# Sums of squares from rows of tokens on ScalarE, and their reciprocal roots spread by products with a diagonal

## The chip, the core and the metric

The kernel runs on one core of one Trainium2 chip. A core has TensorE (PE, with its weight loads PEld), VectorE (DVE), ScalarE (ACT), GpSimd (POOL) and SyncE (SP), which work side by side and wait for each other by semaphores. SP issues nearly all transfers between the memory of the chip (HBM) and the core's own memory. The metric is the device time of one execution in microseconds (us); a kernel's time is the median of its runs.

## The reference

One decoder layer on 512 tokens with 16 learned meta tokens ahead of them, 528 rows of 2048 numbers in float32. What matters here is its first step and what uses it:

```python
def rmsnorm(x, gain):
    xf = x.astype(jnp.float32)
    y = xf * lax.rsqrt(jnp.mean(xf * xf, axis=-1, keepdims=True) + EPS)
    return (y * gain.astype(jnp.float32)).astype(x.dtype)

def hybrid_layer(h, g_pre, w_in, w_gate_up, b_gate, g_gla_out, w_conv, w_out, g_post):
    xn = rmsnorm(h, g_pre)
    p = xn @ w_in
    q, k, v, z_gla, r, hc, gate_b, gate_c, z_conv = jnp.split(p, SPLIT_POINTS, axis=-1)
    ...                      # gated linear attention on q, k, v, r; convolution on the rest
    y = jnp.concatenate([y_gla, y_conv], axis=-1) @ w_out
    return h + rmsnorm(y, g_post)
```

So every token needs one number, the reciprocal root of the mean square of its row of 2048.

## The kernel before

**Layout.** Activations stand transposed: the 2048 features lie on 128 partitions in 16 tiles (k-tiles), the 528 tokens along the free dimension. The input xT comes in that form, and x comes a second time by rows for the residual at the end. Each operand of a product is split into an upper and a lower half, hi and lo, and three products (hi hi, hi lo, lo hi) make one of float32 accuracy. A weight block of 8 k-tiles is a granule: it is loaded into one of five raw buffers, ACT casts the upper half (L145, later L124) and DVE makes the lower (L146, later L125). There are three buffers each for the halves.

**The opening stage.** The loop at L664 loads xT in pieces (`XCUT`: two single k-tiles, then pairs), and the weights of k0 and q0 in between (`WCUT`). For each k-tile ACT writes the upper half of x times the gain (L670, into xa for k-tiles 0 to 7 and xb for 8 to 15) and DVE the lower (L671). For each piece ACT squares the raw tile (L692, L695) and DVE adds it to an accumulator of two tiles (L696). The loop at L697 multiplies k0, q0 and the 16 columns of r for each k-tile. Behind k-tile 10 in the code stands the sum over the partitions: four products of the accumulator with a matrix of ones (L710), which leave the sum of each token's squares on every partition. ACT takes the root of the mean (L711), DVE the reciprocal (L712), and `rstd`, 128 x 528, is the factor of each token on all partitions.

**What needs rstd.** The columns of k, q and r are multiplied by it as DVE takes them out of PSUM (`normal`, L723); r goes through three more steps (L763 to L765). Then DVE normalises the sixteen tiles of xT themselves (L776) while PE does v0, v1, z0 and z1 on the plain halves. From the normalised tiles DVE and ACT make sums and differences of blocks (L783, L788, L789), the operands of the block products (seven instead of eight for a pair of columns) that fill the rest of the kernel. The first pair is z2z3. Its weight blocks are added by DVE (L200, L230) and split (L124, L125).

**What sets the order.** The program is written as one stream, and a scheduling layer orders the instructions of each engine when it is built; the engine then runs its list in that order. Transfers on SP and ACT share eight semaphores in turn: each transfer waits until the one eight before it has landed. SP works in order, so a load that waits holds up those behind it.

**Names.** `scr` is the scratch area that holds the accumulator and the squares, the raw columns of r and the raw gate weights; `ini` is the pool of the opening stage; `st` are the two PSUM banks of the sums; `ident` is the identity matrix, made at the start for transposes.

Of the kernel before, what the change touches and what calls it, by code (L numbers as in the profile page):

```python
# [27 lines left out]
NP = S // P  # L28
# [3 lines left out]
XHALF = L // 2  # L32
# [10 lines left out]


@with_exitstack
def hymba_kernel(ctx, tc, xT, x, g_pre, w_r, w_t, w_up, b_gate, g_gla, w_conv, w_o, g_post, out):
    nc = tc.nc
    PSUM = bass.MemoryType.PSUM

# [12 lines left out]
    def mm(out_, lhsT, rhs, start, stop, **kw):  # L62
        nc.tensor.matmul(out_, lhsT, rhs, start=start, stop=stop, **kw)  # L63

    V, A, G = nc.vector, nc.scalar, nc.gpsimd


    epst = const.tile([P, 1], F32, name="epst")
# [38 lines left out]
    xa = [xap.tile([P, 2, NB, XHALF], F32R, tag=f"xa{i}", name=f"xa{i}") for i in range(2)]  # L107
    WQ = 4 * NB * P
    wr2 = q0w[:, WQ:WQ + KT * 2 * RANK].rearrange("p (k r) -> p k r", r=2 * RANK)
    acc = scr[:, 0:2 * L].rearrange("p (k t) -> p k t", t=L)  # L110
    sqs = [scr[:, L * (2 + 2 * i):L * (4 + 2 * i)].rearrange("p (k t) -> p k t", t=L)
           for i in range(2)]
# [537 lines left out]
    with tc.tile_pool(name="ini", bufs=1, reuse_waits="tile") as ini:  # L650
# [10 lines left out]
        q0v = q0w[:, 0:WQ].rearrange("p (g s k c) -> p g s k c", g=2, s=2, k=NB)  # L661
        wk = [new_gran(), None]
        wq_ = [(q0v[:, g, 0], q0v[:, g, 1], new_raw()) for g in range(2)]
        for n_, (k0, k1) in enumerate(XCUT):  # L664
            ks = slice(k0, k1)
            nc.sync.dma_start(xr[:, ks, :], xT[:, ks, :])
            for kt in range(k0, k1):
                xt, xk = raw_x(kt)
                src = xr[:, kt, :].rearrange("p (s t) -> p s t", t=XHALF)
                A.activation(xt[0][:, :, xk, :], src, AF.Copy, scale=gp[:, kt:kt + 1])  # L670
                V.scalar_tensor_tensor(out=xt[1][:, :, xk, :], in0=src, scalar=gp[:, kt:kt + 1],  # L671
                                       in1=xt[0][:, :, xk, :].bitcast(F32),
                                       op0=ALU.mult, op1=ALU.subtract)
            for a, b in WCUT.get(k0, ()):
                if a == NB:
                    free(wk[0][2])
                    wk[1] = new_gran()
                fill_gran(wk[a // NB], w_t[TILE["k0"]], a, b)
                fill_gran(wq_[a // NB], w_t[TILE["q0"]], a, b)
            if k0 == 0:  # L680
                A.dma_start(wr_raw, w_r)
                V.tensor_copy(wr2[:, :, 0:RANK], wr_raw)
                V.tensor_tensor(out=wr2[:, :, RANK:], in0=wr_raw,
                                in1=wr2[:, :, 0:RANK].bitcast(F32), op=ALU.subtract)
            if k0 == 8:
                nc.sync.dma_start(wup_raw, w_up)
                nc.sync.dma_start(bg, b_gate)
                G.tensor_scalar(out=nbg, in0=bg, scalar1=-1.0, scalar2=None, op0=ALU.mult)
                nc.sync.dma_start(gg, g_gla)
                nc.sync.dma_start(wc, w_conv)  # L690
            if k0 < 2:
                A.activation(acc[:, k0:k1, :], xr[:, ks, :], AF.Square)  # L692
            else:
                sq = sqs[n_ % 2]
                A.activation(sq, xr[:, ks, :], AF.Square)  # L695
                V.tensor_tensor(out=acc, in0=acc, in1=sq, op=ALU.add)  # L696
        for kt in range(KT):  # L697
            xt, xk = raw_x(kt)
            plain_k(k_ps, wk, kt, 0)
            plain_k(q_ps, wq_, kt, NM // 2)  # L700
            for i in range(2):
                for n in range(2):
                    mm(r_ps[n][0:2 * RANK, 0:XHALF], wr2[:, kt, :], xt[i][:, n, xk, :],
                       kt == 0 and i == 0, kt == KT - 1 and i == 1)
            if kt == 10:
                for n in range(2):
                    t = slice(n * XHALF, (n + 1) * XHALF)
                    st_ = bank(f"st{n}")
                    for i in range(2):
                        mm(st_[:, 0:XHALF], ones, acc[:, i, t], i == 0, i == 1)  # L710
                    A.activation(rstd[:, t], st_[:, 0:XHALF], AF.Sqrt, bias=epst, scale=1.0 / D)  # L711
                V.reciprocal(rstd, rstd)  # L712
        for raw in (wk[1][2], wq_[0][2], wq_[1][2]):
            free(raw)

# [313 lines left out]
def _layout(inp):  # L1029
# [9 lines left out]
    return {  # L1039
        "xT": c(h.T[:, COLS].reshape(KT, P, L).transpose(1, 0, 2)),  # L1040
        "x": c(x),
        "g_pre": c(np.asarray(inp["norm_pre"])[0].reshape(KT, P).T),
        "w_r": c(wk[:, :, 3072:3088].transpose(1, 0, 2)),
        "w_t": c(tiles),
# [24 lines left out]
```

## Time and profile before

| | |
|---|---|
| Median of three runs | 821.43 us (820.8 to 821.86) |
| Profiled execution | 823.31 us, its span 820.8 us |
| PE busy | 794.0 us, 97% |
| DVE busy | 688.4 us, 84% |
| ACT busy | 437.6 us, 53% |
| Chain that ended last | PE 77%, DVE 12%, DMA 4%, ACT 4%, issue 2% |
| DMA queue of SP | 94.73 MB, 35.7% of the span |
| Mean granted clock of TensorE | 0.99 |

The span runs from the first to the last instruction of the core; the profiled execution's own time has a few microseconds around it. The change lies in the first 45 us. In the row of 40 slices of 20.5 us each, the DMA digits of the first two slices are 9 and 5 and then mostly 1 to 3: the opening stage is the part in which the transfers are busy. The chain of work that ended last is followed back from the end; its shares say on which engine the end hung, over the whole program.

### The profile page before, as it was taken

How to read it: one execution, taken by the hardware profiler on the slowest of the kernel's cores; microseconds unless marked ns; L12 is line 12 of the kernel's file. 1: busy time of each engine (PE TensorE's matmuls, PEld its weight loads, DVE VectorE, ACT ScalarE, POOL GpSimd, SP SyncE). 2: the span in 40 equal slices, each digit the busy share in tenths (PEclk: the TensorE clock that was granted, in tenths of full speed). 3: DMA queues.
4: the chain of work that ended last, by engine and by line, in shares of the span. 5: the costliest groups of instructions: out<-in, count | busy, mean ns of one | idle time of the engine just before them, and what ended most of it. 6: DMA issues, size and time to landing. Idle time of an engine off the chain costs nothing.

```text
span 820.8 us, 15178 instructions
## 1 busy us (share of the span) xinstructions
PE 794.0 (97%) x6364; PEld 776.2 (95%) x6364; DVE 688.4 (84%) x820; ACT 437.6 (53%) x638; POOL 3.8 (0%) x15
## 2 busy tenths in 40 slices
PE   9999989999999999999999999999999999999992
PEld 8999989998999999999999999999999889999992
DVE  6999979789697789878887888787879986787887
ACT  7635675685766484644444444444446534444442
POOL 0000000000000000000000000000000000000000
PEclk9999999999999999999999999999999999999996
DMA  9513243234133532253333333333333622333346
GB/s 288 223 52 91 92 129 102 89 119 154 54 103 114 169 99 88 85 193 103 111 105 119 100 116 106 115 102 110 105 115 116 178 77 76 104 101 106 103 161 250
DMA packets 34052, 98.97 MB, mean 121 GB/s; under 512 B 4064, under 2 KB 8800, under 8 KB 33344
## 3 DMA queue, kind: packets, MB, share of 16 engines
q1 hardware_dynamic: 31968, 94.73, 35.7%
q10 hardware_dynamic: 2016, 3.29, 1.2%
q8 instruction: 49, 0.80, 0.4%
q14 instruction: 19, 0.16, 0.1%
HBM read 89.61 MB, written 8.39 MB: 119 GB/s over the span
## 4 chain that ended last, share of the span: by engine, by line
PE 77%; DVE 12%; DMA 4%; ACT 4%; issue 2%; SPq 0%; DVEq 0%; ACTq 0%
PE out L63 5%; PE out3P L63 4%; PE out1P L63 4%; PE out2P L63 3%; PE v L63 3%; PE v2v3P L63 3%; PE h0c0P L63 2%; PE h5c5P L63 2%; PE h2c2P L63 2%; PE h7c7P L63 2%; PE h6c6P L63 2%; PE h4c4P L63 2%; PE h3c3P L63 2%; PE h1c1P L63 2%; PE b0s0P L63 2%; PE b6s6P L63 2%
## 5 line engine op out<-in xcount | busy, mean ns | idle before, releaser
L124 ACT CAST whi<-raw 128x1024 fp32r<-128x1024 f32 x225 | 235.2, 1050 | 256.7 <-DVE raw L200 85.4
L125 DVE TENSOR_TENSOR wlo<-raw,whi 128x1024 fp32r<-128x1024 f32 x225 | 273.7, 1220 | 66.7 <-ACT whi L124 61.5
L200 DVE TENSOR_TENSOR raw<-raw 128x1024 f32<-128x1024 f32 x75 | 90.3, 1219 | 6.6 <-DMA raw<-in_w_t_dram 5.6
L230 DVE TENSOR_TENSOR raw<-raw 128x1024 f32<-128x1024 f32 x25 | 30.5, 1220 | 0.6
L145 ACT CAST whi<-raw 128x1024 fp32r<-128x1024 f32 (+2 forms) x13 | 10.9, 845 | 19.5 <-PE v L63 12.8
L63 PE MATMUL out<-whi,xt 128*128 128x512 f32 x64 | 20.0, 394 | 0.0
L63 PE MATMUL out2P<-whi,xt 128*128 128x256 f32 x96 | 17.2, 282 | 0.4 <-ACT whi L124 0.4
L63 PE MATMUL out3P<-whi,xt 128*128 128x256 f32 x96 | 17.2, 282 | 0.4 <-ACT whi L124 0.4
L63 PE MATMUL out1P<-whi,xt 128*128 128x256 f32 x96 | 17.1, 281 | 0.0
L63 PEld LDWEIGHTS out2P<-whi,xt 128*128 128x128 f32 x96 | 14.7, 188 | 0.6 <-ACT whi L124 0.6
L63 PEld LDWEIGHTS out3P<-whi,xt 128*128 128x128 f32 x96 | 14.7, 188 | 0.6 <-ACT whi L124 0.6
L63 PEld LDWEIGHTS out<-whi,xt 128*128 128x128 f32 x64 | 12.0, 188 | 2.8
L63 PEld LDWEIGHTS out1P<-whi,xt 128*128 128x128 f32 x96 | 14.7, 188 | 0.0
L63 PE MATMUL out2P<-wlo,xt 128*128 128x256 f32 x48 | 13.4, 280 | 0.0
L63 PE MATMUL out3P<-wlo,xt 128*128 128x256 f32 x48 | 13.4, 280 | 0.0
L63 PE MATMUL out1P<-wlo,xt 128*128 128x256 f32 x48 | 13.4, 280 | 0.0
L63 PE MATMUL out<-wlo,xt 128*128 128x512 f32 x32 | 12.6, 394 | 0.0
L146 DVE TENSOR_TENSOR wlo<-raw,whi 128x1024 fp32r<-128x1024 f32 (+2 forms) x13 | 12.5, 965 | 0.0
L605 DVE SCALAR_TENSOR_TENSOR y<-hh,wc,y 128x512 f32<-128x512 f32 x16 | 12.0, 748 | 0.2
L363 ACT ACTIVATE junk<-y 128x256 f32<-128x256 f32 x18 | 7.5, 418 | 8.7 <-DVE y L474 8.4
L63 PE MATMUL out3P<-whi,xb 128*128 128x256 f32 x64 | 11.7, 282 | 0.0
L63 PE MATMUL out2P<-whi,xb 128*128 128x256 f32 x64 | 11.6, 282 | 0.0
(749 smaller groups left out, 2701.3 us busy)
## 6 DMA issues: line engine op xcount, KB each, us to landing
raw<-in_w_t_dram SPq DMA_DIRECT2D x108, 512.0 KB, 4.1
raw<-in_w_o_dram SPq DMA_DIRECT2D x24, 512.0 KB, 4.0
raw<-in_w_o_dram SPq DMA_DIRECT2D x16, 256.0 KB, 3.5
xres<-in_x_dram SPq DMA_DIRECT2D x4, 1024.0 KB, 8.0
xr<-in_xT_dram SPq DMA_DIRECT2D x7, 528.0 KB, 6.9
z<-zd SPq DMA_DIRECT2D x8, 256.0 KB, 3.9
yd<-z SPq DMA_DIRECT2D x8, 256.0 KB, 2.0
yg<-yd SPq DMA_DIRECT2D x1, 2048.0 KB, 10.2
```

What stands on the lines that cost most here:

```text
L63: nc.tensor.matmul(out_, lhsT, rhs, start=start, stop=stop, **kw)
L124: A.copy(hi, raw)
L125: V.tensor_tensor(out=lo, in0=raw, in1=hi.bitcast(F32), op=ALU.subtract)
L145: A.copy(hi[:, k, :], raw[:, k, :])
L146: V.tensor_tensor(out=lo[:, k, :], in0=raw[:, k, :], in1=hi[:, k, :].bitcast(F32), op=ALU.subtract)
L200: V.tensor_tensor(out=a, in0=a, in1=b, op=ALU.add)
L230: V.tensor_tensor(out=raw["11"], in0=raw["11"], in1=raw["22"], op=ALU.subtract)
L363: A.activation(junk, oy["src"], AF.Square, accum_out=fin["ssq"][:, t, n:n + 1])
L605: V.scalar_tensor_tensor(out=y, in0=hh[:, i:i + S], scalar=wc[:, j, i:i + 1], in1=y, op0=ALU.mult, op1=ALU.add)
```

## The change

The squares are no longer taken from the transposed tiles. The rows of x, and the meta tokens as a new input `meta`, are loaded a second time during the opening stage: four tiles of 128 tokens and one of 16, each in two halves of 1024 features, into four buffers in the scratch area in turn. ACT squares each half and sums it along the row in the same instruction (`accum_out`), so the sums lie one token a partition in a 128 x 5 x 2 tile. DVE adds the two halves, ACT takes the root, DVE the reciprocal, all on 128 x 5 numbers. ACT then scales the identity by each column, which gives five diagonal matrices, and PE multiplies them by ones: the product has the factor of each token on every partition, in the order of the columns of xT. ACT copies it from PSUM into `rstd`. The seven additions and the reciprocal on 128 x 528 numbers of DVE, and the four products of the squares with ones, are gone.

```diff
-            if k0 < 2:
-                A.activation(acc[:, k0:k1, :], xr[:, ks, :], AF.Square)
-            else:
-                sq = sqs[n_ % 2]
-                A.activation(sq, xr[:, ks, :], AF.Square)
-                V.tensor_tensor(out=acc, in0=acc, in1=sq, op=ALU.add)
+        def square_rows():
+            if not parts:
+                return
+            t, c = parts.pop(0)
+            n = P if t < NP else NM
+            buf = rows[(2 * t + c) % 4][0:n]
+            src = x[t * P:(t + 1) * P] if t < NP else meta
+            nc.sync.dma_start(buf, src[:, c * DH:(c + 1) * DH])
+            A.activation(buf, buf, AF.Square, accum_out=sums[0:n, t, c:c + 1])
...
+            for _ in range(0 if k0 < 2 else 1 if k0 < 8 else 2):
+                square_rows()
...
-            if kt == 10:
+            if kt == 12:
+                V.tensor_tensor(out=rms, in0=sums[:, :, 0], in1=sums[:, :, 1], op=ALU.add)
+                A.activation(rms, rms, AF.Sqrt, bias=epst, scale=1.0 / D)
+                V.reciprocal(rms, rms)
+                for t in range(NP + 1):
+                    A.activation(diag[:, t, :], ident, AF.Copy, scale=rms[:, t:t + 1])
+            if kt == 14:
                 for n in range(2):
-                    t = slice(n * XHALF, (n + 1) * XHALF)
                     st_ = bank(f"st{n}")
-                    for i in range(2):
-                        mm(st_[:, 0:XHALF], ones, acc[:, i, t], i == 0, i == 1)
-                    A.activation(rstd[:, t], st_[:, 0:XHALF], AF.Sqrt, bias=epst, scale=1.0 / D)
-                V.reciprocal(rstd, rstd)
+                    m = slice(NM // 2, NM) if n == 0 else slice(0, NM // 2)
+                    mm(st_[:, 0:NM // 2], ones[0:NM], diag[0:NM, NP, m], True, True)
+                    for t in range(2):
+                        o = NM // 2 + t * P
+                        mm(st_[:, o:o + P], ones, diag[:, 2 * n + t, :], True, True)
+                    A.copy(rstd[:, n * XHALF:(n + 1) * XHALF], st_[:, 0:XHALF])
```

The scheduling layer sets where this stands on each engine. From the second pair of block products on, the lists of all engines are the same as before. Line numbers of the change are higher by 17 to 20 (L670 is L687, L711 and L712 have become L720 to L732, L723 is L743, L776 is L796).

PE at the end of the opening stage; `st0` and `st1` are the banks of the sums, `v00` and `v01` those of v0. Before:

```order
L63 MATMUL k00_129<-xb1_102,whi_179 128x264
L63 MATMUL k01_130<-xb1_102,whi_179 128x264
L63 MATMUL k00_129<-xb0_101,wlo_180 128x264
L63 MATMUL st0_412<-scr_104,ones_88 128x264 x2
L63 MATMUL st1_416<-scr_104,ones_88 128x264 x2
L63 MATMUL k01_130<-xb0_101,wlo_180 128x264
L63 MATMUL q00_131<-xb0_101,q0w_103 128x256
```

In the change:

```order
L63 MATMUL r0_127<-xb1_102,q0w_103 32x264
L63 MATMUL r1_128<-xb1_102,q0w_103 32x264
L63 MATMUL st0_492<-diag_140,ones_88 128x8
L63 MATMUL st0_492<-diag_140,ones_88 128x128 x2
L63 MATMUL st1_497<-diag_140,ones_88 128x8
L63 MATMUL st1_497<-diag_140,ones_88 128x128 x2
L63 MATMUL v00_559<-xa0_108,whi_521 128x264
```

The sums stood in the middle of k-tile 13; the products with the diagonals stand behind the last product of r for k-tile 15, directly ahead of v0.

ACT from the halving of the last pair of k-tiles on. Before:

```order
L695 ACTIVATE scr<-xr 128x1056
L670 ACTIVATE xb_101<-xr,gp 128x2x264 x2
L695 ACTIVATE scr<-xr 128x1056
L145 CAST whi<-raw 128x1024 x2
L711 ACTIVATE rstd<-st_412,epst 128x264
L711 ACTIVATE rstd<-st_416,epst 128x264
L145 CAST whi<-raw 128x1024
L763 CAST rr<-scr 32x528
```

In the change:

```order
L679 ACTIVATE scr,sums<-scr 16x1024
L687 ACTIVATE xb_101<-xr,gp 128x2x264 x2
L679 ACTIVATE scr,sums<-scr 16x1024
L720 ACTIVATE rms<-rms,epst 128x5
L145 CAST whi<-raw 128x1024
L723 ACTIVATE diag<-ident,rms 128x128 x5
L145 CAST whi<-raw 128x1024
L732 COPY rstd<-st_492 128x264
L732 COPY rstd<-st_497 128x264
L145 CAST whi<-raw 128x1024
L783 CAST rr<-scr 32x528
```

The two weight casts of v0 stood behind the last square and ahead of the roots; now one stands between the root and the diagonals and one between the diagonals and the copies.

SP, the loads from k-tiles 8 and 9 on. In the change (before, the three loads of xr behind wc stand together, with nothing in between):

```order
L683 DMA xr_116<-in_xT_dram 128x1056
L703 DMA scr_104<-in_w_up_dram 96x512
L704 DMA bg_84<-in_b_gate_dram 128x4
L706 DMA gg_86<-in_g_gla_dram 128x2
L707 DMA wc_87<-in_w_conv_dram 128x24
L678 DMA scr_104<-in_x_dram 128x1024 x2
L683 DMA xr_116<-in_xT_dram 128x1056
L678 DMA scr_104<-in_x_dram 128x1024 x2
L683 DMA xr_116<-in_xT_dram 128x1056
L678 DMA scr_104<-in_x_dram 128x1024
L678 DMA scr_104<-in_meta_dram 16x1024
L683 DMA xr_116<-in_xT_dram 128x1056
```

Five parts of x and one of meta stand ahead of loads of xr here, three more parts stand ahead of the first row shown, and the second part of meta follows the last. On DVE, the lower halves of v0's two granules (L146) stand ahead of the normalising of r, k and q in both, with the reciprocal of rstd between them before; r is normalised first in the change, where k was first before.

More of the change, by code (lines that the diff above doesn't have):

```diff
@@ L45, in hymba_kernel @@
 @with_exitstack
-def hymba_kernel(ctx, tc, xT, x, g_pre, w_r, w_t, w_up, b_gate, g_gla, w_conv, w_o, g_post, out):
+def hymba_kernel(ctx, tc, xT, x, meta, g_pre, w_r, w_t, w_up, b_gate, g_gla, w_conv, w_o, g_post, out):
     nc = tc.nc
@@ L109, in hymba_kernel @@
     wr2 = q0w[:, WQ:WQ + KT * 2 * RANK].rearrange("p (k r) -> p k r", r=2 * RANK)
-    acc = scr[:, 0:2 * L].rearrange("p (k t) -> p k t", t=L)
-    sqs = [scr[:, L * (2 + 2 * i):L * (4 + 2 * i)].rearrange("p (k t) -> p k t", t=L)
-           for i in range(2)]
+    DH = D // 2
+    rows = [scr[:, o:o + DH] for o in (0, DH, 2 * DH, 9 * L)]
     wr_raw = scr[:, 6 * L:6 * L + KT * RANK].rearrange("p (k r) -> p k r", r=RANK)
@@ L663, in hymba_kernel @@
         wq_ = [(q0v[:, g, 0], q0v[:, g, 1], new_raw()) for g in range(2)]
+        sums = ini.tile([P, NP + 1, 2], F32, name="sums")
+        rms = ini.tile([P, NP + 1], F32, name="rms")
+        diag = ini.tile([P, NP + 1, P], F32, name="diag")
+        G.memset(sums, 0.0)
+        parts = [(t, c) for t in range(NP + 1) for c in range(2)]
+        def square_rows():
[7 more added lines that the diff above has]
+            A.activation(buf, buf, AF.Square, accum_out=sums[0:n, t, c:c + 1])
         for n_, (k0, k1) in enumerate(XCUT):
@@ L1041, in _layout @@
         "x": c(x),
+        "meta": c(np.asarray(inp["meta_tokens"])),
         "g_pre": c(np.asarray(inp["norm_pre"])[0].reshape(KT, P).T),
```

## The prediction

> **What bounds the kernel now.** I read the page first (PE busy for 97% of the span, so a change in the opening stage counts by what it does to the start of the later ones), then the chain of waits from 36 to 100 us, then the stage's timelines engine by engine.
>
> ```profile
> 40.49 23.49 PE v L63 x192
> ...
> 67.54 2.34 DVE tt L783 x2
> ...
> 98.23 1.05 ACT whi L124
> ...
> 99.33 0.74 PE z2z3P L63 x4
> ```
>
> The chain (start, duration, what) runs on PE while it multiplies v, goes over to DVE at 67.5, and comes back to PE at 99.33 through a weight cast of ACT, which had waited for DVE's block sum (L230). PE waits there, and DVE has had no idle time for 55 us before it:
>
> ```profile
> PE z2z3P L63 <- ACT whi L124: 1.0, 1, 1.0
> 43.50:98.10 54.60, 54.60 (x458) 54.57 (x456) 54.59 (x64) 27.20 (x29) 0.53 (x1) 1.00 0.25 78
> ```
>
> The first row is from the waits between 40 and 100 us (total, times, longest), the second from the table of stretches (PE, PEld, DVE, ACT and POOL busy, clock, DMA share, GB/s). DVE is busy for 54.59 of 54.60 us and PE for all of them. So whatever delays DVE's start on this block arrives undiminished at 99 us, on top of the 1.0 us that PE waits already; a delay of PE alone could be at most as large as that of DVE to stay hidden. Behind 99 us both engines follow the same list as before, so a shift there lasts to the end.
>
> The question is thus when the opening stage hands over: when PE starts v, and when DVE starts the normalising at L723 and L776. Its supply is the queue of transfers on SP:
>
> ```profile
> 10.73 0.51 SPq L666 DMA_DIRECT2D xr<-in_xT_dram  x1
> xr<-in_xT_dram SPq DMA_DIRECT2D x1, 528.0 KB, 9.1
> 15.88 0.33 SPq L666 DMA_DIRECT2D xr<-in_xT_dram  x1
> xr<-in_xT_dram SPq DMA_DIRECT2D x1, 528.0 KB, 6.6
> 18.12 0.33 SPq L666 DMA_DIRECT2D xr<-in_xT_dram  x1
> xr<-in_xT_dram SPq DMA_DIRECT2D x1, 528.0 KB, 7.0
> ```
>
> Each pair of rows is one load of two k-tiles of xT: issue time, and us from issue to landing. Pair 8/9 lands at 19.8, pair 10/11 at 22.5, pair 14/15 at 25.1 us. PE takes them up later:
>
> ```profile
> 22.74 0.40 PE L63 MATMUL k<-xb,whi 128*128 128x264 f32 x2
> 26.59 0.29 PE L63 MATMUL k<-xb,whi 128*128 128x264 f32 x1
> 33.28 2.05 PE L63 MATMUL st<-scr,ones 128*128 128x264 f32 x8
> 34.97 0.48 PE L63 MATMUL k<-xb,wlo 128*128 128x264 f32 x1
> 36.47 0.40 PE L63 MATMUL k<-xb,whi 128*128 128x264 f32 x2
> 40.32 0.41 PE L63 MATMUL v<-xa,whi 128*128 128x264 f32 x2
> ```
>
> Pair 8/9 starts at 22.74, 10/11 at 26.59 (3.85 us a pair), 14/15 at 36.47, v at 40.32. The pairs land 2.9, 4.1 and 11.4 us ahead of their use: this is the cover under which added transfers can hide.
>
> **Part 1: the added transfers.** Eight parts of 128 rows x 1024 columns (512 KB) and two of 16 rows enter SP's queue ahead of loads of xT: three parts ahead of pair 8/9, five ahead of 10/11, eight and one small one ahead of 14/15. Rates come from the end of the program, where the same x is read by rows, and from the slowest stretch of the opening stage:
>
> ```profile
> 796.00:798.00 2.00, 2.00 (x20) 2.00 (x19) 1.51 (x3) 1.57 (x4) 0.00 (x0) 1.00 1.03 430
> 798.00:800.00 2.00, 2.00 (x20) 2.00 (x19) 1.98 (x3) 0.39 (x2) 0.00 (x0) 1.00 0.99 418
> 18.00:20.00 2.00, 2.00 (x18) 1.87 (x18) 2.00 (x4) 2.00 (x5) 0.00 (x0) 1.00 1.05 301
> ```
>
> At the first two rows' rate (mean 424 GB/s) a part of 524 kB takes 1.24 us, at the third's 1.74. I take 1.24, for it is the same tensor with rows of the same kind, and keep 1.74 for the range. A small part (64 KB) lies between its bytes, 0.15 us, and 1.24; I take 0.3. The queue's DMA share is 1.05 in that third row, full, so nothing of this goes into gaps: pair 8/9 lands at 19.8 + 3.7 = 23.5, 10/11 at 22.5 + 6.2 = 28.7, 14/15 at 25.1 + 9.9 + 0.3 = 35.3.
>
> The Trainium skill (DMA: Bandwidth & Descriptors, section Bandwidth) sets about 358 GB/s as the limit of HBM for one core. By it a part would take 1.46 us and eight 1.8 us more than in my sum, an estimate from that figure; the rows at 430 and 418 GB/s lie above it and do not bear it out here.
>
> **Part 2: what ACT does with them.** Its rows:
>
> ```profile
> 22.20 0.60 ACT L716 CAST wup<-scr 64x512 fp32r<-64x512 f32 x1
> 27.94 1.35 ACT L670 ACTIVATE xb<-xr,gp 128x528 fp32r<-128x528 f32 x2
> 29.19 1.08 ACT L695 ACTIVATE scr<-xr 128x1056 f32<-128x1056 f32 x1
> 30.17 1.98 ACT L145 CAST whi<-raw 128x1024 fp32r<-128x1024 f32 x2
> 34.47 0.48 ACT L711 ACTIVATE rstd<-st,epst 128x264 f32<-128x264 f32 x1 [2.32 <-PE st L63]
> L985 ACT ACTIVATION_READ_ACCUMULATOR on<-o x12: 194/199/204, 155.4 to 261.2; 128x1 f32 x12
> L987 ACT ACTIVATE ss<-ss,epst x4: 298/298/299, 158.2 to 341.5; 128x4 f32<-128x4 f32 x4
> 159.33 1.55 ACT L990 ACTIVATE on<-o,ss 128x256 f32<-128x256 f32 x4
> ```
>
> Nine squares (seven of 128x1056, two of half that) become ten of 1024 columns. Each has a read of the accumulator of 0.2 us, half of it overlapped: about 1.15 us. The two of 16 rows count in full, since a cast on 64 partitions (0.60 us) is no shorter than two of 128x1024 would make it per column. Ten times 1.15 against 7 x 1.08 + 2 x 0.64: 2.6 us more work on ACT. Most of it falls into waits for the transfers; the tail does not. Pair 12/13 lands one part and one pair ahead of the end of the queue, near 32.5; halving both tiles takes 1.35 (33.9), the last part's square ends at 35.0, the first small one at 36.2, the halving of 14/15 at 37.5, the last small square at 38.7.
>
> **Part 3: PE.** PE wants the upper half of a tile, 0.7 us after its landing. Pair 8/9 starts at 24.2 instead of 22.74; it is done at 28.05, but 10/11 can start only at 29.4, a wait of 1.3. Then 3.85 us a pair: 12/13 at 33.2, 14/15 at 37.1 (its halves are there at 36.9), done at 40.95. Removed on the way: the old sum by ones, 1.7 us (33.28 to 34.97) and the 0.4 us before it. So PE reaches the end of the stage only 0.6 us late.
>
> **Part 4: from the sums to rstd.** This is the new tail. The order of ACT in the change has the square root behind the last small square, a weight cast behind that, and then the five diagonals; the order of PE has the six products behind the last tile and ahead of v. From 38.7: DVE's add (its reciprocal of 128x4 takes 0.17, below; with the handovers 0.2) 38.9, square root 0.3: 39.2, the cast 1.0: 40.2 (its load lands one part after pair 14/15, near 37, so it does not wait), five diagonals. One costs between half and all of the 0.39 us that L990's rows take with twice the columns, together 1.0 to 1.9; I take 1.4: 41.6. The six products have 528 columns where the old four had 1056 in 1.7 us; with the two narrow ones I take 1.0 (0.85 to 1.7): 42.6. v then starts 2.3 us late.
>
> DVE's share:
>
> ```profile
> L988 DVE RECIPROCAL ss<-ss x4: 168/169/171, 158.9 to 342.7; 128x4 f32<-128x4 f32 x4
> L696 DVE TENSOR_TENSOR scr<-scr x7: 1247/1250/1258, 13.6 to 32.0; 128x1056 f32<-128x1056 f32 x7
> 35.88 3.45 DVE L712 RECIPROCAL rstd<-rstd 128x528 f32<-128x528 f32 x1 [0.38 <-ACT rstd L711]
> 39.43 0.84 DVE L723 TENSOR_TENSOR kn<-k,rstd 128x264 f32<-128x264 f32 x3
> 41.59 1.20 DVE L146 TENSOR_TENSOR wlo<-raw,whi 128x1024 fp32r<-128x1024 f32 x1
> 42.83 0.70 DVE L765 TENSOR_TENSOR rr<-scr,rr 32x528 fp32r<-32x528 f32 x1
> 43.54 4.17 DVE L776 SCALAR_TENSOR_TENSOR xr<-xr,gp,rstd 128x528 f32<-128x528 f32 x6
> ```
>
> Removed: seven sums of 1.25 and the reciprocal of 3.45, 12.2 us. They are worth nothing, because they ended at 39.33, beside a stage of PE that ended at 40.3; without them DVE idles. Now DVE waits twice. In ACT's order the second weight cast stands behind the diagonals (41.6 to 42.6), and in DVE's order its remainder (1.2) stands ahead of the normalising, which therefore starts at 43.85 instead of 39.43. ACT copies rstd out (2 x 0.48), casts once more (1.0) and only then makes the two casts of r (0.63 each), until 45.8; DVE, having done r and most of k by 45.4, waits 0.4 for them. With the remaining 2.8 us the first L776 starts at 48.5 instead of 43.54: **+5.0 us**. By the third part nothing behind it gives any of this back.
>
> **The sum.** The profiled execution took 823.31 us, 2.5 more than its span of 820.8. With +5.0 it would be 828.3, the span 825.8. It lies 1.9 above the median of the runs shown, 821.43; the forecast for the median is 826.4.
>
> **Rivals.** (a) Only PE's delay counts: some of DVE's block from 43.5 to 98 is not needed by PE in that order, and +2.3 is left, 823.7. For it: up to 67 us the chain is PE's. Against it: DVE's 54.59 of 54.60, and PE already waiting at 99.
>
> (b) The transfers run as in the slow stretch, 1.74 us a part. Then pair 14/15 lands 4.0 us later, and so does everything behind it: +9, 830.4. For it: the 301 GB/s stand in the very stage into which the parts go. Against it: that stretch holds the small constant loads too. By the Trainium skill's figure (the page above) the time would lie between, near 828.2.
>
> (c) The change is a gain: the parts hide under the cover of 2.9 to 11.4 us, the sum by ones halves, and the reciprocal no longer stands before rstd. Then PE saves 1.7 + 0.4 - 1.0 = 1.1 us and DVE starts as much earlier: 820.3. This needs the pair 10/11 to land by 25.9 for its use at 26.59, so five parts in 3.4 us, below 0.68 us a part, or 770 GB/s. Nothing in the trace moves at that rate.
>
> (d) It does not do what it says in time: rstd is made, but as late as PE ends anyway, and the waits of ACT, PE and DVE in the tail overlap better than in my list. Then +0 to +1.6, 822.2.
>
> **How the numbers follow.** Forecast 0.55, (a) 0.17, (b) 0.13, (c) 0.06, (d) 0.09. The likeliest gives 826.4. The range from 823.2 to 829.2 holds the forecast with its unknown prices (diagonals -0.4 to +0.5, products -0.15 to +0.7, small parts up to +1), (a), and the nearer half of (b). A change of 0.2%, 1.6 us, is about what a measurement of this kernel can tell from none. Slower by more: the forecast, (b) and (a) less 0.02 for a v that starts earlier than worked out, 0.83. Within: 0.08 of (d), half of (c), whose 1.1 us is under the bound, and those 0.02, together 0.13. Faster by more: the other half of (c) and a hundredth of (d), 0.04.
>
> **What would show it.** Right: pair 14/15 landing near 35 us with the queue full until then; PE waiting for tiles near 24 and 28 us; v starting near 42.6; the first L776's successor near 48.5; a wait of 3 to 4 us instead of 1.0 at the products of z2z3 before 104 us. Wrong: L776's successor on time, or late while PE's later waits stay at 1.0 us (then (a)); parts that take under 1 us; or ACT reaching the square root before 38 us.

## The result: slower by 1.05%, and the profile after

| | before | changed |
|---|---|---|
| Median | 821.12 us (820.11 to 821.86, four runs) | 830.42 us (829.59 to 831.97, four runs) |
| Ratio | | 1.0105, 95% interval 1.0086 to 1.0124 |
| Profiled execution | 823.31 us, span 820.8 | 829.95 us, span 828.2 |
| Mean granted clock | 0.990 | 0.991 |

The direction was right, the size was not: forecast 826.4 us, range 823.2 to 829.2. I follow the loss through the trace of the changed kernel in the order of the prediction. First the queue of transfers, SP's issues of the pairs 8/9, 10/11 and 14/15 of xT (issue time; then size and us from issue to landing), as in the prediction:

```profile
15.35 0.33 SPq L683 DMA_DIRECT2D xr<-in_xT_dram  x1
xr<-in_xT_dram SPq DMA_DIRECT2D x1, 528.0 KB, 10.0
23.32 0.33 SPq L683 DMA_DIRECT2D xr<-in_xT_dram  x1
xr<-in_xT_dram SPq DMA_DIRECT2D x1, 528.0 KB, 6.5
30.48 0.48 SPq L683 DMA_DIRECT2D xr<-in_xT_dram  x1
xr<-in_xT_dram SPq DMA_DIRECT2D x1, 528.0 KB, 7.8
```

The pairs land at 25.3, 29.8 and 38.3 us, where the forecast had 23.5, 28.7 and 35.3 and the kernel before 19.8, 22.5 and 25.1. The table of stretches shows why; its last two columns are the DMA share and GB/s:

```profile
20.00:22.00 2.00, 2.00 (x19) 1.90 (x18) 2.00 (x3) 1.21 (x3) 0.00 (x0) 1.00 1.00 299
24.00:26.00 2.00, 0.19 (x2) 0.00 (x0) 0.00 (x0) 1.12 (x4) 0.00 (x0) 1.00 0.91 274
32.00:34.00 2.00, 2.00 (x19) 1.98 (x18) 0.18 (x1) 0.89 (x3) 0.00 (x0) 1.00 1.01 405
8.00:38.00 30.00, 24.90 (x198) 22.80 (x198) 14.40 (x22) 22.14 (x38) 0.60 (x1) 1.00 0.99 336
```

The queue is full (0.99 over 30 us), but its rate goes to and fro between 270 to 300 and 400 GB/s, and the mean is 336, not 424. PE feels it as waits for the halves that ACT makes, 5.7 us in all where the prediction had one wait of 1.3; first PE's two longest stops in its timeline (in brackets the idle time before), then the list of its waits (total, times, longest):

```profile
16.14 0.51 PE L63 MATMUL k<-xa,whi 128*128 128x264 f32 x2 [1.90 <-ACT xa L687]
26.14 0.51 PE L63 MATMUL k<-xb,whi 128*128 128x264 f32 x2 [1.95 <-ACT xb L687]
```

```profile
PE k L63 <- ACT xb L687: 3.2, 3, 2.0
PE k L63 <- ACT xa L687: 2.5, 2, 1.9
```

Then the tail, in the timelines of ACT, PE and DVE:

```profile
39.93 1.04 ACT L679 ACTIVATE scr<-scr 16x1024 f32<-16x1024 f32 x1
41.36 0.30 ACT L720 ACTIVATE rms<-rms,epst 128x5 f32<-128x5 f32 x1 [0.30 <-DVE rms L719]
42.50 1.57 ACT L723 ACTIVATE diag<-ident,rms 128x128 f32<-128x128 f32 x5
44.12 1.98 PE L63 MATMUL st<-diag,ones 16*128 16x8 f32 x12 [0.33 <-ACT diag L723]
45.86 0.49 PE L63 MATMUL v<-xa,whi 128*128 128x264 f32 x2
46.18 0.86 DVE L743 TENSOR_TENSOR scr<-r,rstd 32x264 f32<-32x264 f32 x3
50.61 2.12 DVE L796 SCALAR_TENSOR_TENSOR xr<-xr,gp,rstd 128x528 f32<-128x528 f32 x3
```

Last square, root, diagonals, products, v, normalising and the first product that followed L776: the order is the predicted one, each item two to three us later than predicted. v starts at 45.86 instead of 40.32, DVE's large products at 50.61 instead of 43.54, **7.07 us late**. The delay arrives where the kernel before waited once for 1.0 us; PE's waits there and its timeline:

```profile
PE z2z3P L63 <- ACT whi L124: 2.2, 2, 1.2
PE z2z3P L63 <- DVE wlo L125: 0.5, 1, 0.5
```

```profile
107.40 0.58 PE L63 MATMUL z2z3P<-xt,whi 128*128 128x256 f32 x1 [0.99 <-ACT whi L124]
```

The product that started at 99.33 starts at 107.40, 8.07 us later. From there to the end of the span it is 720.8 us, and was 721.5 before. So the whole loss is there by this one product, 7.07 us of it by the end of the opening stage. I use it as the marker below.

### The profile page after: what moved, and what is told of

Read it like the earlier page. It is cut to its first block, busy times and chain, and to the rows that moved or that the text cites. A ratio compares the mean times of both kernels' runs of the same rounds, so it can differ in the third digit from the quotient of the medians.

```text
span 828.2 us, 15214 instructions
## 1 busy us (share of the span) xinstructions
PE 794.8 (96%) x6368; PEld 775.4 (94%) x6368; DVE 678.5 (82%) x814; ACT 442.6 (53%) x655; POOL 2.9 (0%) x16
## 4 chain that ended last, share of the span: by engine, by line
PE 75%; DVE 12%; ACT 5%; DMA 4%; issue 3%; DVEq 0%; SPq 0%; ACTq 0%
PE out L63 5%; PE out1P L63 4%; PE out2P L63 3%; PE out3P L63 3%; PE v L63 3%; DMA xr<-in_xT_dram 3%; PE v2v3P L63 2%; PE k3q3P L63 2%; PE h0c0P L63 2%; DVE wlo L125 2%; PE h7c7P L63 2%; PE h4c4P L63 2%; PE h1c1P L63 2%; PE h6c6P L63 2%; PE h5c5P L63 2%
## 5 line engine op out<-in xcount | busy, mean ns | idle before, releaser
L146 DVE TENSOR_TENSOR wlo<-raw,whi 128x1024 fp32r<-128x1024 f32 (+2 forms) x13 | 12.6, 973 | 3.3 <-ACT whi L145 3.3
L688 DVE SCALAR_TENSOR_TENSOR xb<-xr,gp,xb 128x528 fp32r<-128x528 f32 x8 | 5.8, 766 | 10.9 <-ACT xb L687 10.9
L688 DVE SCALAR_TENSOR_TENSOR xa<-xr,gp,xa 128x528 fp32r<-128x528 f32 x8 | 5.9, 766 | 9.7 <-ACT xa L687 9.7
L679 ACT ACTIVATE scr<-scr 128x1024 f32<-128x1024 f32 (+1 forms) x10 | 10.5, 1052 | 3.1 <-DMA scr<-in_x_dram 3.1
```

The lines of the kernel that those rows point to most:

```text
L146: V.tensor_tensor(out=lo[:, k, :], in0=raw[:, k, :], in1=hi[:, k, :].bitcast(F32), op=ALU.subtract)
L679: A.activation(buf, buf, AF.Square, accum_out=sums[0:n, t, c:c + 1])
```

## The experiments

Theory: the added transfers make pair 14/15 and the last squares late, DVE starts its block late, and nothing behind gives that back. Rivals: the new tail (casts, diagonals, products) is itself the loss; only PE's delay counts (rival (a) of the prediction). A second question came with the result: why a part costs more than 1.24 us. For each run the table has the landing of pair 14/15, DVE's first product on the tiles of xT, the z2z3P product behind PE's last wait there (all us, from the profiled execution), the median less that of the kernel before that was timed beside it, and the ratio.

| Run | 14/15 | DVE | z2z3P | us | ratio (95%) |
|---|---|---|---|---|---|
| before | 25.1 | 43.5 | 99.3 | | |
| the change | 38.3 | 50.6 | 107.4 | +9.3 | 1.0105 (1.0086 to 1.0124) |
| again, timed | 38.4 | 50.9 | 107.7 | +9.3 | 1.0106 (1.0081 to 1.0130) |
| again, one execution | 39.1 | 51.7 | 108.5 | +10.7 | none |
| 1 no row loads | 25.1 | 43.5 | 99.8 | +0.7 | 1.0005 (0.9993 to 1.0018) |
| 2 loads only | 37.9 | 54.7 | 109.6 | +11.1 | 1.0124 (1.0098 to 1.0151) |
| 3 rows last | 25.1 | 52.1 | 109.9 | +10.5 | 1.0126 (1.0103 to 1.0149) |
| 4 half the loads | 32.9 | 47.3 | 103.8 | +4.3 | 1.0055 (1.0038 to 1.0072) |
| 5 DVE delayed | 24.6 | 49.3 | 104.0 | +5.9 | 1.0069 (1.0045 to 1.0093) |
| 6 PE delayed | 25.2 | 44.0 | no wait | +5.1 | 1.0051 (1.0034 to 1.0067) |
| 7 sums on POOL | 25.9 | 49.0 | 109.7 | +10.7 | 1.0125 (1.0102 to 1.0149) |
| 8 parts reversed, one execution | 37.3 | 51.3 | 109.9 | +10.7 | none |
| 9 one part, one execution | 35.7 | 48.2 | 105.0 | +5.5 | none |
| 9 one part, timed | 36.8 | 49.3 | 106.1 | +7.3 | 1.0080 (1.0054 to 1.0107) |
| 10 whole blocks | 36.8 | 49.2 | 106.0 | +7.2 | 1.0079 (1.0053 to 1.0105) |
| 11 POOL's queue | 32.5 | 53.1 | 110.3 | +11.4 | 1.0130 (1.0093 to 1.0167) |
| 12 the same, paced | 33.9 | 55.8 | 112.7 | +13.1 | 1.0147 (1.0121 to 1.0173) |

Wherever z2z3P is waited for, its shift against 99.3 and the shift of the time agree within 1.5 us: the later the marker, the slower the kernel, whatever made it late. (DVE's column is not the same point in all: in runs 2 and 5 one lower half of weights more (L146) stands ahead of that product, in run 7 two of the products stand ahead of the normalising of k.)

### 1. The change without its transfers

```diff
-            src = x[t * P:(t + 1) * P] if t < NP else meta
-            nc.sync.dma_start(buf, src[:, c * DH:(c + 1) * DH])
-            A.activation(buf, buf, AF.Square, accum_out=sums[0:n, t, c:c + 1])
+            have = xr[0:n, ks, :].rearrange("p k t -> p (k t)")[:, 0:DH]
+            A.activation(buf, have, AF.Square, accum_out=sums[0:n, t, c:c + 1])
...
-                square_rows()
+                square_rows(ks)
```

> The change without its transfers: the ten squares read columns of the xT pair that is loaded already, so the sums are of the wrong numbers and the row loads are left out; squares, diagonals, products and the new order stay. Theory (the transfers delay the stage, the tail rides on their end): pair 14/15 lands near 25 us again, v starts within 1 us of 40.3, DVE's first L776 starts near 43.5 to 45, the time is 820 to 823, +1.5 at most against before. Rival (the new tail of square root, casts, diagonals and products is itself the loss): +4 or more, with DVE's block still starting near 48.

Ratio 1.0005: no loss is left, and no gain. Timelines of PE and DVE:

```profile
36.45 1.98 PE L63 MATMUL st<-diag,ones 16*128 16x8 f32 x12
38.19 0.49 PE L63 MATMUL k<-xb,whi 128*128 128x264 f32 x2
...
39.95 0.64 PE L63 MATMUL v<-xa,whi 128*128 128x264 f32 x4
43.50 3.48 DVE L795 SCALAR_TENSOR_TENSOR xr<-xr,gp,rstd 128x528 f32<-128x528 f32 x5
```

The tail is all there, but early, beside PE's last tiles, and DVE's block starts where it always did (43.54 before). The rival of the tail falls. The same rows show that the 12.2 us less of DVE's work are worth nothing even where nothing else is in the way, and they price the products: the next matmul of k starts 1.74 us after the first of them.

### 2. The kernel before with the loads alone

```diff
...
+            src = x[t * P:(t + 1) * P] if t < NP else x[0:NM]
+            nc.sync.dma_start(extra[(2 * t + c) % 4][0:n], src[:, c * DH:(c + 1) * DH])
...
+            for _ in range(0 if k0 < 2 else 1 if k0 < 8 else 2):
+                load_rows()
```

> The kernel before, with the ten loads of rows put into the queue at the places of the change, into buffers that nothing reads; the sums are made as before. Theory (the transfers carry the loss): pair 14/15 lands near 38 us, the accumulated squares are complete near 40, the old reciprocal of 3.45 us follows it, and the time is +8 to +10, no better than the change. Rival (the new tail is the cause): less than +4. If the extra price of a part (1.6 us in place of 1.24) belongs to these loads and not to what uses them, the landings agree with those of the change within 1 us.

The loads alone cost as much as the whole change; by the medians more, but the two intervals touch. Pair 14/15 lands at 37.9, 0.3 from the change, so the price of a part belongs to the loads and not to the squares that use them. DVE's timeline shows why this kernel ends later still:

```profile
45.80 3.44 DVE L728 RECIPROCAL rstd<-rstd 128x528 f32<-128x528 f32 x1
54.66 1.44 DVE L792 SCALAR_TENSOR_TENSOR xr<-xr,gp,rstd 128x528 f32<-128x528 f32 x2
```

The accumulated squares are complete only with the last pair, and the long reciprocal, which the change has made short, then stands on the path (DVE's block starts at 54.7, in the change at 50.6). The change spares that reciprocal, but in a stage that the loads have already made late.

### 3. The rows behind all of xT

```diff
-            for _ in range(0 if k0 < 2 else 1 if k0 < 8 else 2):
-                square_rows()
+        for _ in range(2 * NP + 2):
+            square_rows()
```

> The change, with all ten loads of rows behind pair 14/15 in the queue and their squares behind the last halving: PE is not starved of tiles, but rstd comes as late as in the change. Theory (what counts is how late DVE starts its block, and PE's start of v follows the products of the tail): +7 to +9, as in the change, with PE waiting once, ahead of the products, instead of at each pair. Rival (a) of the prediction (the delay of PE by the starved tiles is what counts): +3 or less.

PE gets its tiles as in the kernel before and is done with them by 38.7 us, and still +10.5. PE's timeline and the table of stretches (clock third from the end):

```profile
45.55 3.41 PE L63 MATMUL st<-diag,ones 16*128 16x8 f32 x12 [6.90 <-ACT diag L723]
```

```profile
45.00:47.00 2.00, 1.45 (x6) 1.42 (x6) 0.82 (x2) 2.00 (x4) 0.00 (x0) 0.50 0.79 279
51.00:53.00 2.00, 2.00 (x18) 2.00 (x18) 1.99 (x6) 0.22 (x1) 0.00 (x0) 1.00 0.74 248
```

One wait of 6.9 us ahead of the products takes the place of the many. Starved tiles are therefore not needed for the loss; a late rstd is enough. The size is not clean: behind the wait PE ran at a granted clock of 0.50 for about 5 us, and the products took 3.41 us instead of 1.98. The Trainium skill (TensorE: Matmul & The Clock Gate, section What's actually happening) states that PE's clock falls to half behind an idle window of about 3.4 us. The trace agrees in that 6.9 us did it, but shorter waits did it too. The clock was 0.50 in the change from 107.0 to 110.4 us, behind waits of 1.2 and 1.0 us, and in the kernel before from 122.4 to 125.8, behind one of 2.1. Rows of the change, then of the kernel before:

```profile
107.00:110.00 3.00, 2.60 (x12) 2.60 (x13) 3.00 (x4) 1.57 (x3) 0.00 (x0) 0.50 0.47 158
```

```profile
122.50:125.50 3.00, 3.00 (x16) 3.00 (x15) 3.00 (x7) 2.07 (x4) 0.00 (x0) 0.50 0.59 175
```

In all traces here the granted clock changes only in steps of 3.41 us, and in the change timed again the same two waits of 1.2 and 1.0 us left it at 1.00. That points to how a wait falls on these steps; it differs between executions of one kernel.

### 4. Half the transfers

```diff
-            nc.sync.dma_start(buf, src[:, c * DH:(c + 1) * DH])
-            A.activation(buf, buf, AF.Square, accum_out=sums[0:n, t, c:c + 1])
+            have = rows[2 * t % 4][0:n]
+            if c == 0:
+                nc.sync.dma_start(have, src[:, 0:DH])
+            A.activation(buf, have, AF.Square, accum_out=sums[0:n, t, c:c + 1])
```

> The change with half of its transfers: the second half of each set of rows is not loaded, and the square of it is taken of the first half again (the sums are of the wrong numbers). Theory (the loss is the bytes in the queue, less the cover in front of their use): pair 14/15 lands 5 to 7 us later than in the kernel before instead of 13, v starts 0 to 1.5 us late, the time is +0.5 to +3. Rival (any added transfer in the queue costs in proportion, without cover): half of the change's loss, +4 to +5.

+4.3, about half the loss, as the rival had it, and the pair at 32.9, later than the theory put it (5 to 7 us late; it is 7.8). It still does not tell cover from proportion, because the edit has a wait of its own: only two of the four buffers are loaded, and the load of the small part waited for the squares of one of them.

```profile
28.66 0.33 SPq L680 DMA_DIRECT2D scr<-in_meta_dram  x1
```

```profile
28.00:30.00 2.00, 2.00 (x19) 1.97 (x18) 0.70 (x2) 2.00 (x5) 0.00 (x0) 1.00 0.32 119
```

SP, which works in order, issued nothing from 24.7 to 28.7 us, and the queue ran dry (DMA share 0.32 from 28 to 30).

### 5 and 6. A delay of DVE alone, and one of PE alone

Both start from the kernel before and add no transfer.

```diff
                 V.reciprocal(rstd, rstd)
+                for _ in range(4):
+                    V.tensor_tensor(out=acc, in0=acc, in1=rstd.unsqueeze(1).broadcast_to([P, 2, L]),
+                                    op=ALU.mult)
```

> The kernel before, with four multiplications of 128x1056 on DVE (about 1.25 us each, 5 us) behind the reciprocal, on a buffer that is dead by then; no transfer is added and PE has no more to do. Theory (DVE is full from 43.5 to 98 us and a delay of it passes to the end undiminished): +4 to +5. Rival (a) (some of DVE's block is not needed by PE in that order): less than +1.5.

```diff
                 V.reciprocal(rstd, rstd)
+        more = bank("more")
+        for _ in range(16):
+            mm(more[:, 0:XHALF], ones, acc[:, 0, 0:XHALF], True, True)
```

> The kernel before, with sixteen more products of 128x264 on PE ahead of v (0.21 us each, 3.4 us), which nothing reads; DVE has no more to do and its start does not depend on them. Theory (PE is full from 40 to 98 us, and waits 1.0 there): of the 3.4 us the wait of 1.0 takes up 1.0, and +2.4 is left; later waits of DVE's make may give back up to 2 more. Rival (DVE alone decides what comes at 98 us): +0.5 or less.

The rows of the first are DVE's added work (1.24 to 1.26 us a product, 5.0 in all), its block and PE's waits from 40 to 110 us; those of the second PE's added work, v, and PE's only waits from 40 to 160 us:

```profile
39.32 1.26 DVE L714 TENSOR_TENSOR scr<-scr,rstd 128x1056 f32<-128x1056 f32 x1
49.28 3.48 DVE L779 SCALAR_TENSOR_TENSOR xr<-xr,gp,rstd 128x528 f32<-128x528 f32 x5
```

```profile
PE z2z3P L63 <- ACT whi L124: 2.9, 4, 1.2
PE z2z3P L63 <- DVE wlo L125: 1.5, 2, 0.8
```

```profile
40.74 7.28 PE L63 MATMUL more<-scr,ones 128*128 128x264 f32 x32
47.66 0.60 PE L63 MATMUL v<-xa,whi 128*128 128x264 f32 x2
```

```profile
PE k1q1P L63 <- DVE wlo L125: 2.1, 2, 1.7
```

With PE untouched (v at 40.20), 5.0 us of DVE's work cost 5.7 by the ratio (3.7 to 7.6): they arrive in full, and PE's waits at z2z3P grow from 1.0 to 4.4. Rival (a) falls. In the other run I had counted each product once; the trace has two records for each (32 for 16), so the delay was 6.9 us instead of 3.4. It cost 4.2 by the ratio (2.8 to 5.5): the wait at z2z3P is gone, and 2.7 us of the delay (1.4 to 4.1) were taken up. That wait was 1.0; what took up the rest isn't shown. Part of it may be the clock, which stayed at 1.00 here where the kernel before had its 3.4 us at 0.50. A late PE is thus forgiven in part, a late DVE not, as the prediction's reading of 54.59 busy us in 54.60 said.

### 7. DVE freed without a transfer

```diff
-                V.tensor_tensor(out=acc, in0=acc, in1=sq, op=ALU.add)
+                G.tensor_tensor(out=acc, in0=acc, in1=sq, op=ALU.add)
```

> The kernel before, with the seven sums of squares of 128x1056 made by POOL in place of DVE; nothing else, no added transfer. POOL does nothing in this stage otherwise. This keeps the one part of the change that costs no transfer: DVE rid of 8.8 us of sums. The planner then puts two of the L776 products ahead of the normalising of k. Theory (DVE's start decides what comes at 98 us, and PE waits there 1.0 us and later 2.1 us): if POOL needs at most 2.5 us a sum, rstd comes no later, DVE's block starts 1 to 2 us earlier and the time is 0.5 to 2 us below the kernel before. Rival (the end of the opening stage on PE decides, so that a lead of DVE is worth nothing): within 0.4 us of before. Third way: POOL needs over 3.3 us a sum, or slows DVE, the last sum comes after 36 us and the time is +2 or more.

This was meant as a version faster than both; it is the third way, +10.7. Timelines of POOL (four sums), DVE (the lower halves of one pair) and PE:

```profile
23.54 11.49 POOL L696 TENSOR_TENSOR scr<-scr 128x1056 f32<-128x1056 f32 x4
29.82 5.78 DVE L671 SCALAR_TENSOR_TENSOR xb<-xr,gp,xb 128x528 fp32r<-128x528 f32 x2
32.80 0.81 PE L63 MATMUL k<-xb,whi 128*128 128x264 f32 x2 [5.17 <-DVE xb L671]
```

POOL's 2.5 to 2.9 us a sum are little over what I had allowed. But DVE's two products, 1.44 us in the kernel before, take 5.78: each takes as long as a sum of POOL beside it. The Trainium skill (SBUF — State Buffer, section Who interferes with whom) states the rule: a DVE instruction with two inputs in SBUF contends with a GpSimd instruction that reads SBUF, by an exclusive lock. The trace agrees: 2.9 us a product, the length of one sum. PE stood still for 5.2 us, and its clock was 0.50 for 3.4 us behind that.

### 8 to 12. What a part costs

Pair 14/15 lands 13.2 us later than before, for eight large parts and a small one. With 0.3 for the small one a part costs 1.61 us; over the four traces with the same ten loads in SP's queue (the change three times and run 2: 37.9 to 39.1) it is 1.57 to 1.72. That is what a part costs the queue, not what it takes itself. By the distance between landings the eight parts took 11.2, 12.8 and 13.3 us in the three traces of the change (9.9 forecast), and six weight loads of 256 KB between them 7.5, 6.6 and 6.8 where they took 5.9 before: some of the extra falls on other loads. Single parts are not all dear. In the change the sixth is issued at 25.40, the seventh at 26.20:

```profile
scr<-in_x_dram SPq DMA_DIRECT2D x1, 512.0 KB, 5.7
scr<-in_x_dram SPq DMA_DIRECT2D x1, 512.0 KB, 7.2
```

The sixth lands at 31.1, 1.3 us after pair 10/11 (29.8), the seventh at 33.4, 2.3 us after the sixth. The next runs asked what makes the difference: the change once more, the parts in another order (run 8), one source for all (9), unbroken blocks (10), and another queue (11, 12).

> The change once more, unaltered, for a second trace. If the stretches in which the queue moves only 220 to 310 GB/s belong to places of the program, the seventh part of the rows takes over 2 us again (2.33 in the first trace) and the sixth about 1.27; pair 14/15 lands within 0.5 us of 38.25. If they fall by chance, other transfers are slow, and pair 14/15 still lands between 36.5 and 39.5.

> The change once more, timed beside the kernel with the one part: 830.4 within 1.5 us, pair 14/15 between 37 and 39.5.

```diff
-        parts = [(t, c) for t in range(NP + 1) for c in range(2)]
+        parts = [(t, c) for t in (3, 2, 1, 0, 4) for c in range(2)]
```

> The change with the four sets of rows loaded in reverse order (rows 384 to 511 first), all else the same. If the slow transfers belong to the addresses of those rows in memory, the first two parts take over 1.5 us each and the seventh and eighth 1.3 at most. If they belong to the time or the place in the queue, the seventh and eighth are slow again (2.3 and 1.6). The time is that of the change within 2 us either way.

```diff
-            src = x[t * P:(t + 1) * P] if t < NP else meta
-            nc.sync.dma_start(buf, src[:, c * DH:(c + 1) * DH])
+            src = x[0:P] if t < NP else meta
+            nc.sync.dma_start(buf, src[:, 0:DH] if t < NP else src[:, c * DH:(c + 1) * DH])
```

> The change with all eight large parts read from the same 128 rows and 1024 columns of x (the sums are of the wrong numbers), so that all of them come from one 512 KB of memory. If reading ever new rows of x is what makes a part take 1.6 us, each takes 1.24 to 1.3 here, pair 14/15 lands at 35.3 to 36 and the time is 3 us below the change. If not, the landings are those of the change within 1 us.

> The kernel with all eight large parts read from the same 128 rows and 1024 columns, timed beside the change: the first look gave 827.58 us and pair 14/15 at 35.65. If it is the new rows of memory that make a part dearer, it is 2 us or more below the change of the same call, and pair 14/15 lands by 36.5 again. If the first look was chance, it is within 1 us of the change and pair 14/15 lands between 37 and 39.

```diff
-            src = x[t * P:(t + 1) * P] if t < NP else meta
-            nc.sync.dma_start(buf, src[:, c * DH:(c + 1) * DH])
+            i = 2 * t + c
+            src = (x[64 * i:64 * (i + 1)].rearrange("r (h d) -> (r h) d", h=2) if t < NP
+                   else meta[:, c * DH:(c + 1) * DH])
+            nc.sync.dma_start(buf, src)
```

> The change with each large part read as one unbroken block of 512 KB (64 whole rows of x, a half row on each partition) in place of half of 128 rows that lie 8 KB apart; bytes, places in the queue and buffers are the same (the sums are then of other rows, so the factors are wrong). If the strided reading makes parts take 1.6 us and more, all take 1.24 to 1.3, pair 14/15 lands at 35.3 to 36 and the time is 827 or less. If it does not, some parts take 1.6 to 2.5 again, pair 14/15 lands between 37 and 39.5 and the time is 829.5 to 832.

In run 8 SP waited 5.1 us for ACT to free the buffer of the small part, so its landing at 37.3 isn't only the price of the parts. In all four traces of the change and of the reversed order the seventh part, measured from the landing ahead of it, is slow (2.33, 2.04, 2.26 and 2.16 us), and in run 2 too (2.55; in two of them the sixth as well), though it is other rows in the reversed order: the slow part goes with the place, not with the address. In the three traces that read one part again and again or unbroken blocks it took 1.29 each time, and pair 14/15 landed at 35.7 to 36.8, ahead of all five others; but in two of the three the third part was slow instead (2.68 and 2.13). That points to the strided reading of ever new memory as a part of the extra, about 1.5 us of it; the ratios (1.0079 and 1.0080 against 1.0105 and 1.0106) point the same way, but their intervals overlap, so it isn't shown. The rest of it is in none of these: from 20 to 24 us the queue moves 276 to 331 GB/s in each of them. Rows of the change, timed again, and then of the whole blocks:

```profile
20.00:22.00 2.00, 2.00 (x18) 1.87 (x17) 1.70 (x3) 1.02 (x3) 0.00 (x0) 1.00 1.00 317
```

```profile
20.00:22.00 2.00, 2.00 (x18) 1.98 (x18) 1.04 (x3) 0.71 (x2) 0.00 (x0) 1.00 1.08 299
```

The other queue: POOL, idle in this stage, issues the ten loads, in run 11 as soon as the buffers allow, in run 12 each behind a copy of one column (the first added line, in run 12 alone; `kl` is a k-tile of an earlier pair, handed over by the caller) that waits for that pair.

```diff
-            nc.sync.dma_start(buf, src[:, c * DH:(c + 1) * DH])
+            G.tensor_copy(buf[:, 0:1], xr[0:n, kl, 0:1])
+            nc.gpsimd.dma_start(buf, src[:, c * DH:(c + 1) * DH])
```

> The change with its ten loads issued by POOL, which is idle in this stage, in place of SP, so that they stand in a queue of their own and the loads of xT no longer behind them. If a slow stretch is that of one queue, with two of them the rate stays at 400 GB/s or more and pair 14/15 lands by 36, the time is 827 or less. If all transfers share one rate, the total is as late (all of xT and rows in by 37 to 39), the pairs land in another order, and the time is within 3 us of the change.

> The ten loads issued by POOL in a queue of their own, each behind a copy of one column that waits for an earlier pair of xT, so that they come at about the pace of the change. If the slow stretches belong to the one queue of the change, the rate stays near 400 GB/s from 18 to 36 us, pair 14/15 lands by 34 and the last row by 37, and the time is 1 to 4 us below the change (826.5 to 829.5). If they belong to the transfers as such, the rate falls to 270 to 320 GB/s in part of that time, all rows are in by 38 to 40 and the time is that of the change within 1.5 us.

Stretches from 8 to 38 us, first of POOL's queue, then paced:

```profile
8.00:38.00 30.00, 25.12 (x194) 24.15 (x195) 13.99 (x21) 21.32 (x38) 3.74 (x7) 0.94 1.03 378
```

```profile
8.00:38.00 30.00, 25.08 (x182) 23.33 (x181) 12.42 (x19) 18.63 (x33) 7.33 (x22) 0.94 1.02 371
20.00:22.00 2.00, 0.00 (x0) 0.00 (x0) 0.61 (x1) 1.01 (x2) 0.72 (x2) 1.00 1.05 307
```

Two queues moved 371 and 378 GB/s, one trace each, where the one queue of the change moved 327 to 337. The paced kernel still fell to 307 at 20 us, and run 11 to 257 at 22, so the slow stretch doesn't belong to the one queue either. Both are slower than the change: PE stood still for up to 3.1 and 3.5 us early on, with the clock at 0.50 for 3.4 us behind it, and DVE's first product came at 53.1 and 55.8. In run 11 the last row landed at 38.8, as in the change (38.6), but PE's order has the products with the diagonals ahead of the last k-tile there; how much each of these costs isn't shown. What makes the slow stretches stays open.

## Why the prediction was wrong in size and right in kind

**What bounds it, right.** That DVE's start of the block counts, undiminished, and that nothing behind it gives it back, is shown by runs 5 and 6 and by the marker. Taking away the sums and the long reciprocal is worth nothing (run 1). The order of the tail was as listed.

**Part 1, 1.24 us a part: the step that failed.** It measured 1.61 (1.57 to 1.72), which put pair 14/15 at 38.3 instead of 35.3 and the last small square's end at 41.0 instead of 38.7; PE's tiles came late with it, and v 5.5 us late instead of 2.3. The price was taken from two rows at the end of the program, "for it is the same tensor with rows of the same kind", and the slow row of the stage (18 to 20 us, 301 GB/s) was laid to the small constant loads and called the slowest stretch, which it isn't. Rows of the kernel before that I had not put beside it:

```profile
8.00:10.00 2.00, 1.43 (x9) 1.21 (x10) 1.53 (x3) 1.86 (x5) 0.00 (x0) 1.00 0.97 290
10.00:12.00 2.00, 2.00 (x19) 1.94 (x18) 1.72 (x3) 1.47 (x4) 0.00 (x0) 1.00 0.98 328
8.00:25.00 17.00, 16.43 (x131) 15.58 (x132) 15.71 (x22) 16.29 (x27) 1.51 (x1) 1.00 1.02 353
```

From 8 to 12 us there are no small constant loads, and it is as slow. The mean of the full queue in the stage itself was 353 GB/s: 1.48 us a part, 12.2 us in all, a landing at 37.3. That was the price to take, though still a little below what was measured (1.57 to 1.72, 37.9 to 39.1). The Trainium skill's figure of about 358 GB/s (DMA: Bandwidth & Descriptors, section Bandwidth) would have given nearly the same, though not as the limit that it is called there: the stretches lie now above, now below it.

When by luck the pair did land at 35.7 (run 9, one execution), DVE's first product started at 48.2, forecast 48.5, and the time was +5.5, forecast +5.0. So the rest of the chain was sized well, but for two small terms.

**Part 4, the products: 1.0 us.** 1.74 in run 1 and in the change, just above the bounds given (0.85 to 1.7): six products, two of them narrow, cost PE what the old four did. The diagonals took 1.57 instead of 1.4. v came at 45.9 instead of 42.6.

**Part 4, DVE's share.** The first product 50.6 instead of 48.5, +7.1 for +5.0; another 1.0 was lost up to z2z3P (+8.1), where DVE was busy for 53.66 of 54.40 us and no longer without a gap. PE's waits there were 2.2 and 0.5, not 3 to 4, since PE itself came 5.5 us late.

**The sum.** In the profiled executions the loss was 6.6 us (7.4 in the span) against 5.0. The step from there to the median took off 1.9, the excess of the one execution before. The changed kernel's profiled execution lies 0.5 below its median, and that of before 2.2 above the median of its runs now, so 2.7 of the 9.3 are scatter between single executions and medians. Some of it goes with the granted clock: of the executions of the kernel before that were timed beside the runs, the eleven at 0.993 have a median of 821.3 us, the five at 0.990, the clock of the profiled one, 822.6. Of the 4.0 us that the forecast missed, some 1.6 are the loss in the trace and 2.4 this conversion.

**Rivals.** (a) fell with run 5, (c) with run 1: without any transfer the change is no gain. (d) fell too, the tail was later than listed, not better overlapped. (b) named the time, 830.4, and the right term; its 1.74 us a part was above what was measured, and its +9 for the trace is +7.4. It had a chance of 0.13, and the range held only its nearer half. That cut was the mistake: the only row for the rate in that very stage spoke for (b).

**Range.** 830.42 lies above 829.2. With the price of a part between the two rows, 1.24 and 1.74, both ends kept, it would have reached 830.4.

## What to carry to other kernels

Price an added transfer by the mean rate of the stage into which it goes, over all its stretches in which the queue is full, not by the best rows of another stage. Before taking work off an engine, look at what it would do with the time: here DVE lost 12 us of work and started no earlier. A delay has to be followed to the first product that two engines' lists meet at; whichever engine has no gap up to there passes it on in full.

## What the runs showed of the chip that I had not expected

- Within one queue of transfers that is all but always full, stretches of 270 to 320 GB/s and of 400 to 412 alternate. From 20 to 26 us all three traces of the change are slow, elsewhere not always the same stretches, and neither the order of the rows of x nor the one queue alone makes them (runs 8, 11 and 12). By the distance between landings single transfers of 512 KB take 1.25 to 1.7 us or, a few times in a stage, 2.0 to 2.8.
- With a second queue the mean was 371 and 378 GB/s instead of 327 to 337, one trace each, and the kernel was still slower.
- A sum of 128x1056 on POOL (2.5 to 2.9 us) holds up a product on DVE for its whole length: 2.9 us instead of 0.72.
- Behind 6.9 us of idleness PE ran at a clock of 0.50 for about 5 us. Behind one wait of 2.1 us, or two of 1.2 and 1.0, it ran at 0.50 for 3.4 us in some executions and not in others; the clock changed only in steps of 3.41 us.
